# Sparse-attention softmax in a hybrid decoder trunk: scaling the attention outputs in place of the probabilities

## The chip, the core and the metric

The kernel runs on one NeuronCore of a Trainium2 chip. Five engines work side by side: TensorE (PE in the profile; its weight loads have a row of their own, PEld), VectorE (DVE), ScalarE (ACT), GpSimd (POOL) and SyncE (SP), which issues most DMA transfers. The metric is the device time of one execution in microseconds (us). The kernel before has a median of 1512.5 us in 3 runs (1512.34 to 1512.63).

## What is computed

Two decoder layers over 512 tokens of width 1024. A layer has one input projection, three head groups side by side (RWKV-7 recurrence, causal pooling, sparse attention), one output projection, a gated ConvFFN and a gated per-layer embedding. The change concerns the attention group, 8 query heads on 2 key/value heads of width 64. With 512 tokens the selected branch takes in every causal block and the window branch every causal key, so both are plain causal softmax attention with their own keys and values:

```
ps = softmax(where(ok_s, q . k_sel, -1e30));  o_sel = ps @ v_sel
pw = softmax(where(ok_w, q . k_win, -1e30));  o_win = pw @ v_win
pc = softmax(where(ok_c, q . k_cmp, -1e30)) * any(ok_c);  o_cmp = pc @ v_cmp
o  = sigmoid(g0) * o_cmp + sigmoid(g1) * o_sel + sigmoid(g2) * o_win
```

Per query and head, a causal branch thus needs its exponentials, their sum, and one factor: gate over sum.

## The kernel before, in words

Activations lie feature-major (features on partitions, the 512 tokens along the row). Large projections are made of three products of rounded halves per 128 weights, 128x512 each (lines 159 to 161).

The attention stage of a layer works on 8 units of work, one for each block `c` of 128 queries and each half `jp` of the heads. A unit has four heads: `j2` (2) times key/value head `g` (2). The stage is three pieces of code:

- `scores(c, j, pbs)`: for each `g` and branch `ty` (selected, window), two products and a causal mask go into a PSUM tile `sc` (lines 760 to 762 for c < 2, 770 to 772 for c of 2 and 3; two buffers), VectorE takes the row maximum `smax` (764, 773), and ScalarE writes the exponentials into `pb` and their row sums into `ssum` (776). Then `fac` = gate / sum (781, 782), and line 787 multiplies each `pb` by its factor, one number for each query, which here is the partition: three of four products on VectorE, one on GpSimd.
- `values(c, jp, pbs)`: TensorE transposes each 128x128 piece of the probabilities (860, PSUM tile `ptp`, two buffers of the tag `mm`), ScalarE copies four of them out as `zt` (862), and `weigh` multiplies by the values (868) into PSUM tile `o`, of which there is one. Both branches and the compressed branch (873, from `ptb`, whose probabilities carry their factor already) add up in the same 256 columns. ScalarE then writes `yh` from it (885) and VectorE the rounding rest `yl` (886).
- `pair` runs `scores` for the two heads j of a unit; the loop over `work` hands out the scores of unit i+1 while `values` of unit i is emitted.

The RWKV recurrence (lines 499 to 569) and the pooling run in the same stretch on the same engines, and the output projection `wo` follows, which reads `yh` and `yl` of all groups. What order each engine's queue has in the end is set at build time by a scheduler with its own clock; tiles come from pools with a fixed number of buffers, and a tile waits for a free one.

Of the kernel before, what the change touches and what calls it, by code (L numbers as in the profile page):

```python
# [15 lines left out]
P = 128  # L16
# [14 lines left out]
# parameter columns  # L31
PG_MIX, PG_FFN, PG_PLE, PMU, PW0, PA0, PKK, PKA, PRK, PGNG, PGNB, PSC, PC0, PC1, PC2, PCB, NPAR = (
    0, 8, 16, 24, 32, 34, 36, 38, 40, 42, 44, 46, 48, 92, 136, 180, 224)
# constant columns
C_ID, C_XM, C_BO, C_CM, C_VM, C_SEL, C_SGN, C_INV, C_HALF, C_ONE, C_FLAG, C_PIW, C_PFX, NCST = (
    0, 128, 256, 384, 512, 640, 642, 643, 644, 660, 661, 665, 667, 699)
# masks that pass through a temporary
C_DM, C_SCAN, NMSK = 0, 128, 640

# order of the feature-major tiles of the input projection  # L40
# [3 lines left out]
def hybrid(tc, xT, pT, pos, cst, msk, par, gfin, w_in, w_tok, w_out, w_up, w_down, w_pg, w_pp,  # L44
# [5 lines left out]
    with ctx:  # L50
# [85 lines left out]
        class Pace:  # L136
            """hands out the pieces of a second stream of work while the first one is emitted"""
# [17 lines left out]
        def gemm(ps, chunks):  # L155
            """chunks: list of (whi, wlo, xhi, xlo)"""
# [7 lines left out]
        def wtile(src, ps, xs, name, lo_eng=None):  # L164
            """one 128-wide tile of outputs: K chunks of weights against the list xs of (hi, lo)"""
            gemm(ps, wchunks(src, xs, lo_eng))
# [91 lines left out]
        # ================================================================  # L258
        for l in range(L):
# [5 lines left out]
            # derived parameters  # L265
# [20 lines left out]
            def mixed(i, dst):  # L286
                """token shift of tile i into dst"""
# [15 lines left out]
            # ---- RWKV: decay, a, gate  # L303
# [35 lines left out]
            # ---- normalised keys  # L339
# [12 lines left out]
            # k * (1 + (a - 1) k_a)  # L352
# [13 lines left out]
            for hp in range(2):  # L366
# [5 lines left out]
                # 2 a kk  # L372
# [5 lines left out]
            # token shift of the values  # L378
# [8 lines left out]
            # pairwise products within a chunk  # L387
# [19 lines left out]
            # the bonus  # L407
# [4 lines left out]
            # inverse of the unit triangular matrices: substitution in 32-blocks, instance on partition,  # L412
            # even columns on the lower half of the partitions and odd ones on the upper half
# [52 lines left out]
            # token-major [B|K] scaled by the chunk's decay, and V  # L466
# [24 lines left out]
            # one chunk of the recurrence  # L491
# [112 lines left out]
            # stacks of the compressed branch's inputs: even positions on the lower half, odd ones on the upper half  # L604
# [19 lines left out]
            # token-major values and gates  # L624
# [24 lines left out]
            # compressed keys and values  # L649
# [12 lines left out]
            # key stacks for the compressed branch  # L662
# [12 lines left out]
            # values of the compressed branch on (j, g, n) rows, zero outside their group  # L675
# [20 lines left out]
            # scores of the compressed branch: (head, block) on partitions, then transposed  # L696
# [47 lines left out]
            def scores(c, j, pbs):  # L744
                w = (c + 1) * P
                smax = small([P, 2, 2], "smax", 3)
                ssum = small([P, 2, 2], "ssum", 3)
# [3 lines left out]
                for g in range(2):  # L751
# [26 lines left out]
                    if g == 0:  # L778
                        yield
                fac = small([P, 2, 2], "fac", 3)  # L780
                V.reciprocal(fac, ssum)
                V.tensor_tensor(fac, fac, GT[:, c, 8:24].rearrange("p (a h) -> p h a", h=8)[:, j * 2:j * 2 + 2, :],
                                op=ALU.mult)
                for g in range(2):
                    for ty in range(2):
                        e = G if (g, ty) == (j % 2, 1) else V
                        e.tensor_scalar(pbs[g][:, ty, 0:w], pbs[g][:, ty, 0:w], fac[:, g, ty:ty + 1], None, op0=ALU.mult)
# [380 lines left out]
```

## Time and profile before

| What | Value |
|---|---|
| Time, median of 3 runs | 1512.5 us |
| Profiled execution: span from first to last instruction | 1509.1 us |
| PE busy | 1456.7 us (97%) |
| DVE, ACT, POOL busy | 824.0, 680.7, 741.9 us |
| Attention stage of layer one / two | 184 to 299.3 / 922 to 1036.5 us |

The profile names an instruction by line, engine and tile. "Busy" of PE counts modelled ends of pipelined products, so a busy PE is not one at its full rate. A wait is put down to the instruction that released it.

### The profile page before, as it was taken

How to read it: one execution, taken by the hardware profiler on the slowest of the kernel's cores; microseconds unless marked ns; L12 is line 12 of the kernel's file. 1: busy time of each engine (PE TensorE's matmuls, PEld its weight loads, DVE VectorE, ACT ScalarE, POOL GpSimd, SP SyncE). 2: the span in 40 equal slices, each digit the busy share in tenths (PEclk: the TensorE clock that was granted, in tenths of full speed). 3: DMA queues.
4: the chain of work that ended last, by engine and by line, in shares of the span. 5: the costliest groups of instructions: out<-in, count | busy, mean ns of one | idle time of the engine just before them, and what ended most of it. 6: DMA issues, size and time to landing. Idle time of an engine off the chain costs nothing.

```text
span 1509.1 us, 21414 instructions
## 1 busy us (share of the span) xinstructions
PE 1456.7 (97%) x7762; PEld 1165.4 (77%) x7762; DVE 824.0 (55%) x1362; ACT 680.7 (45%) x1302; POOL 741.9 (49%) x621
## 2 busy tenths in 40 slices
PE   6998999999999999999999989899999999999997
PEld 4786766588888888888877877656888888888886
DVE  7769687425773155522567696862277712554234
ACT  5552365544443244443544524664354423444433
POOL 3354553274555455556613554523645554555653
PEclk9999999999999999999999999999999999999998
DMA  5233400042223322333431343001322333223332
GB/s 174 67 98 93 119 16 3 15 140 89 99 92 98 103 95 95 96 97 107 137 109 55 97 126 85 1 15 57 125 91 98 94 97 102 98 98 93 97 101 94
DMA packets 79945, 134.70 MB, mean 89 GB/s; under 512 B 11104, under 2 KB 21856, under 8 KB 79840
## 3 DMA queue, kind: packets, MB, share of 16 engines
q1 hardware_dynamic: 78688, 132.29, 28.1%
q8 instruction: 61, 1.00, 0.3%
q10 hardware_dynamic: 1152, 1.05, 0.2%
q14 instruction: 44, 0.36, 0.1%
HBM read 120.59 MB, written 4.19 MB: 83 GB/s over the span
## 4 chain that ended last, share of the span: by engine, by line
PE 85%; DVE 10%; ACT 2%; issue 1%; DMA 1%; POOL 0%; SPq 0%; DVEq 0%; ACTq 0%
PE up L161 11%; PE up L160 11%; PE up L159 11%; PE dn L160 5%; PE dn L161 5%; PE dn L159 5%; PE z L161 3%; PE z L159 3%; PE z L160 3%; PE o L868 2%; PE ptp L860 2%; PE wo L159 2%; PE wo L160 2%; PE wo L161 2%; PE pg L159 2%; PE pg L160 2%
## 5 line engine op out<-in xcount | busy, mean ns | idle before, releaser
L133 POOL TENSOR_TENSOR wlo<-raw,whi 128x512 fp32r<-128x512 f32 (+3 forms) x392 | 508.0, 1300 | 478.3 <-ACT whi L132 450.8
L132 ACT CAST whi<-raw 128x512 fp32r<-128x512 f32 (+3 forms) x440 | 261.1, 596 | 437.0 <-PE up L160 111.4
L159 PE MATMUL up<-xhl,whi 128*128 128x512 f32 x704 | 274.1, 389 | 0.0
L161 PE MATMUL up<-xhl,wlo 128*128 128x512 f32 x704 | 273.7, 389 | 0.0
L160 PE MATMUL up<-xhl,whi 128*128 128x512 f32 x704 | 273.6, 389 | 0.0
L159 PEld LDWEIGHTS up<-xhl,whi 128*128 128x128 f32 x704 | 132.2, 188 | 27.4
L160 PEld LDWEIGHTS up<-xhl,whi 128*128 128x128 f32 x704 | 132.2, 188 | 27.4
L161 PEld LDWEIGHTS up<-xhl,wlo 128*128 128x128 f32 x704 | 132.2, 188 | 27.2
L159 PE MATMUL dn<-ghl,whi 128*128 128x512 f32 x352 | 136.9, 389 | 0.0
L160 PE MATMUL dn<-ghl,whi 128*128 128x512 f32 x352 | 136.9, 389 | 0.0
L161 PE MATMUL dn<-ghl,wlo 128*128 128x512 f32 x352 | 136.3, 389 | 0.0
L159 PE MATMUL z<-xhl,whi 128*128 128x512 f32 x288 | 118.1, 411 | 6.4 <-ACT whi L132 5.7
L160 PE MATMUL z<-xhl,whi 128*128 128x512 f32 x288 | 117.9, 410 | 5.6 <-DVE xhl L192 5.6
L931 DVE SCALAR_TENSOR_TENSOR cv<-cv,par 128x511 f32<-128x511 f32 x88 | 78.1, 888 | 82.0 <-ACT cv L930 82.0
L161 PE MATMUL z<-xhl,wlo 128*128 128x512 f32 x288 | 117.7, 409 | 4.9 <-DVE wlo L133 4.7
L946 DVE TENSOR_TENSOR x<-x,dn 128x512 f32<-128x512 f32 x32 | 22.0, 688 | 166.7 <-PE dn L161 166.7
L933 DVE SCALAR_TENSOR_TENSOR cv<-cv,par 128x510 f32<-128x510 f32 x88 | 100.4, 1142 | 2.9
L929 DVE TENSOR_TENSOR cv<-up,rb 128x512 f32<-128x512 f32 x88 | 60.0, 683 | 73.8 <-PE up L161 59.6
L776 ACT ACTIVATE pb<-sc,smax 128x128 f32<-128x128 f32 (+3 forms) x128 | 66.9, 531 | 41.9 <-DVE smax L764 20.3
L930 ACT ACTIVATE cv<-cv,par 128x512 f32<-128x512 f32 x88 | 71.6, 815 | 31.0 <-DVE cv L929 31.0
L159 PEld LDWEIGHTS dn<-ghl,whi 128*128 128x128 f32 x352 | 66.1, 188 | 13.8
L160 PEld LDWEIGHTS dn<-ghl,whi 128*128 128x128 f32 x352 | 66.1, 188 | 13.7
(302 smaller groups left out, 2634.4 us busy)
## 6 DMA issues: line engine op xcount, KB each, us to landing
raw<-in_w_up_dram SPq DMA_DIRECT2D x176, 256.0 KB, 2.6
raw<-in_w_in_dram SPq DMA_DIRECT2D x72, 256.0 KB, 2.8
raw<-in_w_down_dram SPq DMA_DIRECT2D x64, 256.0 KB, 2.6
raw<-in_w_out_dram SPq DMA_DIRECT2D x32, 256.0 KB, 2.7
raw<-in_w_pg_dram SPq DMA_DIRECT2D x32, 256.0 KB, 2.6
raw<-in_w_down_dram SPq DMA_DIRECT2D x32, 192.0 KB, 2.3
x<-in_xT_dram SPq DMA_DIRECT2D x16, 256.0 KB, 3.6
qs<-hl SPq DMA_DIRECT2D x32, 128.0 KB, 2.3
```

The costliest lines, as they stand in the source:

```text
L132: S.copy(hi[:, :ncol], raw[:, :ncol])
L133: (lo_eng or G).tensor_tensor(lo[:, :ncol], raw[:, :ncol], hi[:, :ncol].bitcast(F32), op=ALU.subtract)
L159: TE.matmul(ps, wh, xh, start=i == 0, stop=False)
L160: TE.matmul(ps, wh, xl, start=False, stop=False)
L161: TE.matmul(ps, wl, xh, start=False, stop=i == n - 1)
L776: S.activation(pb[:, ty, 0:w], srcs[ty], AF.Exp, bias=smax[:, g, ty:ty + 1], accum_out=ssum[:, g, ty:ty + 1])
L860: TE.transpose(ps[:, (g * 2 + j2) * P:(g * 2 + j2 + 1) * P], pbs[j2][g][:, ty, kb * P:(kb + 1) * P], ident)
L868: TE.matmul(op_[g * 64:g * 64 + 64, 0:256], VT[:, kb, ty * 128 + g * 64:ty * 128 + g * 64 + 64], pts[ty][:, g, :], start=False, stop=kb == ...
L929: V.tensor_tensor(u_, ps, rb, op=ALU.mult)
L930: S.activation(c_, u_, AF.Identity, scale=pc(PC2 + n), bias=pc(PCB + n))
L931: V.scalar_tensor_tensor(c_[:, 1:T], u_[:, 0:T - 1], pc(PC1 + n), c_[:, 1:T], op0=ALU.mult, op1=ALU.add)
L933: V.scalar_tensor_tensor(c_[:, 2:T], u_[:, 0:T - 2], pc(PC0 + n), c_[:, 2:T], op0=ALU.mult, op1=ALU.add)
```

## The change

The probabilities keep their raw exponentials: line 787 goes. One `ssum` and one `fac` tile serve the four heads of a unit. TensorE multiplies each column of `fac`, repeated 64 times as weights, by the identity, which spreads the factors along a row for all 64 partitions of a head (PSUM tile `fb` in the tag `sc` of the scores); ScalarE copies `fb` to SBUF. In `values` the two branches go to separate halves of `o`; VectorE multiplies `o` by `fb`, adds the halves and adds the compressed branch. That branch has its own products now, `oc`, for two query blocks at once, ahead of the units (PSUM tag `o`, copied by ScalarE). `ptb` moves from pool tag `x` to `p`, and `oc` takes its place. Comments go too, which shifts line numbers.

```diff
-            def scores(c, j, pbs):
+            def scores(c, j, pbs, ssum):
...
-                    if g == 0:
-                        yield
-                fac = small([P, 2, 2], "fac", 3)
-                V.reciprocal(fac, ssum)
-                V.tensor_tensor(fac, fac, GT[:, c, 8:24].rearrange("p (a h) -> p h a", h=8)[:, j * 2:j * 2 + 2, :],
-                                op=ALU.mult)
-                for g in range(2):
-                    for ty in range(2):
-                        e = G if (g, ty) == (j % 2, 1) else V
-                        e.tensor_scalar(pbs[g][:, ty, 0:w], pbs[g][:, ty, 0:w], fac[:, g, ty:ty + 1], None, op0=ALU.mult)
-                yield
+                    yield
 
             def pair(c, jp, pbs):
+                ssum = small([P, 4, 2], "ssum", 3)
                 for j2 in range(2):
                     pbs.append([])
-                    yield from scores(c, jp * 2 + j2, pbs[j2])
+                    yield from scores(c, jp * 2 + j2, pbs[j2], ssum[:, j2 * 2:j2 * 2 + 2, :])
+                fac = small([P, 4, 2], "fac", 3)
+                V.reciprocal(fac, ssum)
+                V.tensor_tensor(fac, fac, GT[:, c, 8:24].rearrange("p (a h) -> p h a", h=8)[:, jp * 4:jp * 4 + 4, :],
+                                op=ALU.mult)
+
+                fp = psum("fb", "sc")
+                for ty in range(2):
+                    for j2 in range(2):
+                        for g in range(2):
+                            TE.matmul(fp[g * 64:g * 64 + 64, (ty * 2 + j2) * P:(ty * 2 + j2 + 1) * P],
+                                      fac[:, j2 * 2 + g, ty:ty + 1].to_broadcast([P, 64]), ident, start=True, stop=True)
+                fb = unit([P, 2, 256], "fb", tag="p")
+                S.copy(fb.rearrange("p a q -> p (a q)"), fp)
+                pbs.append(fb)
...
-                ptb = unit([P, 2, 2, 2, P], "ptb", tag="x")
+                ptb = unit([P, 2, 2, 2, P], "ptb", tag="p")
...
+                oc = unit([P, 2, 2, 256], "oc", tag="x")
+                for jp in range(2):
+                    ps = psum("oc", "o")
+                    for g in range(2):
+                        TE.matmul(ps[g * 64:g * 64 + 64, :], VC[:, g * 64:g * 64 + 64], ptb[:, jp].rearrange("p c j q -> p (c j q)"),
+                                  start=True, stop=True)
+                    S.copy(oc[:, jp].rearrange("p c q -> p (c q)"), ps)
+                OC.append(oc)
...
-                            TE.matmul(op_[g * 64:g * 64 + 64, 0:256],
+                            TE.matmul(op_[g * 64:g * 64 + 64, ty * 256:(ty + 1) * 256],
...
-                for g in range(2):
-                    TE.matmul(op_[g * 64:g * 64 + 64, 0:256], VC[:, g * 64:g * 64 + 64],
-                              PTB[c // 2][:, c % 2, jp].rearrange("p j q -> p (j q)"), start=True, stop=False)
...
-                ov = op_[:, 0:256].rearrange("p (j q) -> p j q", q=P)
+                ob = small([P, 2, 256], "nacc", 1)
+                V.tensor_tensor(ob.rearrange("p a q -> p (a q)"), op_, pbs[2].rearrange("p a q -> p (a q)"), op=ALU.mult)
+                V.tensor_tensor(ob[:, 0, :], ob[:, 0, :], ob[:, 1, :], op=ALU.add)
+                V.tensor_tensor(ob[:, 0, :], ob[:, 0, :], OC[c // 2][:, jp, c % 2, :], op=ALU.add)
+                ov = ob[:, 0, :].rearrange("p (j q) -> p j q", q=P)
```

Where the queues move, place one: TensorE at the end of the first unit's scores in layer one. `tpc` are the transposes of the compressed probabilities, `yt` and `g` belong to the recurrence. Before:

```order
L760 MATMUL sc_1942<-ku_1713,qs_1412 128x256 [waits DVE_49,Activation_49]
L761 MATMUL sc_1942<-ku_1714,qs_1412 128x256
L762 MATMUL sc_1942<-cstr 128x256
L811 MATMUL tpc_2095<-cst,pcs_1682 128x128 [waits DVE_49,Activation_49]
L811 MATMUL tpc_2095<-cst,pcs_1682 128x128 x3
```

After:

```order
L759 MATMUL sc_1934<-ku_1713,qs_1412 128x256 [waits DVE_49,Activation_49]
L760 MATMUL sc_1934<-ku_1714,qs_1412 128x256
L761 MATMUL sc_1934<-cstr 128x256
L793 MATMUL fb_1950<-cst,fac_1947 64x128 [waits DVE_49,Activation_49]
L793 MATMUL fb_1950<-cst,fac_1947 64x128 x7
L815 MATMUL tpc_2094<-cst,pcs_1682 128x128 [waits Activation_49]
L815 MATMUL tpc_2094<-cst,pcs_1682 128x128 x3
```

The eight products of `fb` now stand between the last scores and `tpc`, and they wait for VectorE's `fac`.

Place two: TensorE at the end of the stage, where the last unit's values meet the output projection `wo`, whose first product with that unit's `yh` (line 159) is the last row. Before:

```order
L161 MATMUL wo_3014<-yh_689,wlo_3018 128x512
L868 MATMUL o_2888<-zt_2948,vt_921 64x256 [waits Activation_49]
L868 MATMUL o_2888<-zt_2948,vt_921 64x256
L159 MATMUL wo_2970<-yh_690,whi_2973 128x512 [waits Activation_49]
L159 MATMUL wo_3014<-yh_690,whi_3017 128x512
```

After:

```order
L161 MATMUL wo_3040<-yh_689,wlo_3044 128x512
L879 MATMUL o_2912<-zt_2970,vt_921 64x256 [waits Activation_49]
L879 MATMUL o_2912<-zt_2970,vt_921 64x256
L159 MATMUL wo_2996<-yh_690,whi_2999 128x512 [waits Activation_49]
L159 MATMUL wo_3040<-yh_690,whi_3043 128x512
```

Nothing has moved in between `o` and `wo` on TensorE. VectorE's queue for the same two last units, after:

```order
L893 TENSOR_TENSOR nacc_2892<-nacc_2892 128x256 [waits DVE_49]
L786 TENSOR_TENSOR fac_2898<-fac_2898,gt_922 128x8 [waits DVE_49]
L894 TENSOR_TENSOR nacc_2892<-nacc_2892,oc_2119 128x256 [waits DVE_49]
L898 TENSOR_TENSOR yl_693<-nacc_2892,yh_689 128x2x128 [waits Activation_49]
L892 TENSOR_TENSOR nacc_2985<-o_2912,fb_2910 128x512 [waits DVE_49,PE_49,Activation_49]
L893 TENSOR_TENSOR nacc_2985<-nacc_2985 128x256 [waits DVE_49]
L894 TENSOR_TENSOR nacc_2985<-nacc_2985,oc_2119 128x256 [waits DVE_49]
L898 TENSOR_TENSOR yl_694<-nacc_2985,yh_690 128x2x128 [waits Activation_49]
```

Three dependent instructions (892 to 894) now stand between `o` and `yl`; before, `yl_694<-o_2888,yh_690` stood alone.

## Rows read from the trace of the kernel before

**Rows 1.** Stage halves by window: start:end, length, busy PE, PEld, DVE, ACT, POOL, clock, DMA
```profile
184.00:245.00 61.00, 54.63 (x438) 39.02 (x438) 51.18 (x140) 37.87 (x124) 31.64 (x41) 0.97 0.10 29
245.00:299.30 54.30, 51.32 (x349) 31.51 (x345) 27.88 (x66) 31.24 (x75) 11.39 (x8) 1.00 0.04 11
922.00:984.00 62.00, 55.92 (x474) 39.59 (x473) 53.89 (x147) 38.52 (x125) 30.98 (x43) 1.00 0.05 15
984.00:1036.50 52.50, 50.30 (x344) 30.78 (x340) 26.52 (x62) 31.24 (x74) 10.83 (x8) 1.00 0.04 11
```
**Rows 2.** Waits from 184 to 299.3 us: total us, times, longest
```profile
PEld sc L770 <- ACT pb L776: 3.7, 6, 1.4
...
PEld ptp L860 <- DVE pb L787: 1.7, 5, 0.4
...
PEld ptp L860 <- POOL pb L787: 0.7, 2, 0.4
```
**Rows 3.** The same from 922 to 1036.5 us
```profile
PEld sc L770 <- ACT pb L776: 4.8, 9, 1.2
...
PEld ptp L860 <- DVE pb L787: 1.7, 4, 0.7
...
PEld ptp L860 <- POOL pb L787: 0.4, 1, 0.4
```
**Rows 4.** Groups of the span: out<-in xcount | busy us, mean ns | idle before, releaser
```profile
L873 PE MATMUL o<-ptb,VC 128*64 128x256 f32 x64 | 10.4, 400 | 1.9 <-DVE fac L782 0.7 <-DVE yl L886 0.6 <-ACT ptb L815 0.4
L787 DVE TENSOR_SCALAR pb<-pb,fac 128x128 f32<-128x128 f32 (+3 forms) x96 | 46.2, 533 | 0.7 <-DVE fac L782 0.2
L862 ACT COPY zt<-ptp 128x512 f32<-128x512 f32 x80 | 45.7, 587 | 36.6 <-PE o L868 20.4 <-PE ptp L860 16.2
L787 POOL TENSOR_SCALAR pb<-pb,fac 128x128 f32<-128x128 f32 (+3 forms) x32 | 40.1, 1253 | 66.5 <-DVE fac L782 48.5 <-ACT zt L862 12.4 <-DVE sb L529 4.0
L946 DVE TENSOR_TENSOR x<-x,dn 128x512 f32<-128x512 f32 x32 | 22.0, 688 | 166.7 <-PE dn L161 166.7
L782 DVE TENSOR_TENSOR fac<-fac,gt 128x4 f32<-128x4 f32 x32 | 6.4, 199 | 0.7
L781 DVE RECIPROCAL fac<-ssum 128x4 f32<-128x4 f32 x32 | 5.5, 172 | 6.0 <-ACT pb L776 5.6
```
**Rows 5.** TensorE in order of time: start, us, form, count
```profile
248.85 0.60 PE L536 MATMUL y<-sb,ar 128*64 128x128 f32 x4
...
289.01 0.71 PE L860 MATMUL ptp<-cst,pb 128*128 128x128 f32 x5
289.65 0.65 PE L868 MATMUL o<-zt,vt 128*64 128x256 f32 x4
290.24 0.66 PE L860 MATMUL ptp<-cst,pb 128*128 128x128 f32 x4
...
295.50 1.08 PE L868 MATMUL o<-zt,vt 128*64 128x256 f32 x8
```
**Rows 6.** All engines at the end of the first unit's scores
```profile
190.38 1.75 PE L811 MATMUL tpc<-cst,pcs 128*128 128x128 f32 x7 [1.54 <-ACT pb L776]
...
190.81 0.21 ACT L776 ACTIVATION_READ_ACCUMULATOR pb<-sc,smax 128x1 f32 x1
...
190.85 0.18 DVE L782 TENSOR_TENSOR fac<-fac,gt 128x4 f32<-128x4 f32 x1
```
**Rows 7.** A window just there, columns as in rows 1
```profile
190.00:200.00 10.00, 9.62 (x84) 7.81 (x84) 6.63 (x23) 7.19 (x24) 4.06 (x6) 0.83 0.09 29
```
**Rows 8.** All engines at the end of layer one's stage
```profile
298.11 0.65 PE L868 MATMUL o<-zt,vt 128*64 128x256 f32 x4
298.81 0.37 ACT L885 CAST yh<-o 128x256 fp32r<-128x256 f32 x1 [1.97 <-PE o L868]
...
299.24 0.73 PE L159 MATMUL wo<-yh,whi 128*128 128x512 f32 x2 [0.47 <-ACT yh L885]
```
**Rows 9.** VectorE: two dependent products of 128x256, one after the other
```profile
217.16 0.41 DVE L566 TENSOR_TENSOR ysq<-ysq,bo 128x256 f32<-128x256 f32 x1
217.60 0.42 DVE L567 TENSOR_TENSOR ysq<-ysq,gg 128x256 f32<-128x256 f32 x1
```

More of the change, by code (lines that the diff above doesn't have):

```diff
@@ L742, in hybrid @@
                     nc.sync.dma_start(KU[g][1][b, ty, :].bitcast(F32), hl[a, 0, :].bitcast(F32))
-            def scores(c, j, pbs):
+            def scores(c, j, pbs, ssum):
                 w = (c + 1) * P
                 smax = small([P, 2, 2], "smax", 3)
-                ssum = small([P, 2, 2], "ssum", 3)
                 ps = None
@@ L802, in hybrid @@
             pace.tick(1000.0)
-            PTB = []
+            OC = []
             for cp2 in range(2):
                 pcs, ei = PCS[cp2]
-                ptb = unit([P, 2, 2, 2, P], "ptb", tag="x")
+                ptb = unit([P, 2, 2, 2, P], "ptb", tag="p")
                 after(G.memset(ptb, 0.0), ei)
@@ L814, in hybrid @@
                     a = slice(j2 * 64, j2 * 64 + 64)
-                    S.copy(ptb[a, :, :, j2, :].rearrange("p c h q -> p (c h) q"),
-                           tps[a, :].rearrange("p (x q) -> p x q", q=P))
-                PTB.append(ptb)
+                    S.copy(ptb[a, :, :, j2, :].rearrange("p h c q -> p c h q"),
+                           tps[a, :].rearrange("p (c h q) -> p c h q", c=2, q=P))
+                oc = unit([P, 2, 2, 256], "oc", tag="x")
[6 more added lines that the diff above has]
+                OC.append(oc)
             def pooling(i):
@@ L867, in weigh @@
                         for g in range(2):
-                            TE.matmul(op_[g * 64:g * 64 + 64, 0:256],
+                            TE.matmul(op_[g * 64:g * 64 + 64, ty * 256:(ty + 1) * 256],
                                       VT[:, kb, ty * 128 + g * 64:ty * 128 + g * 64 + 64],
-                                      pts[ty][:, g, :], start=False, stop=kb == c and ty == 1)
-                for g in range(2):
-                    TE.matmul(op_[g * 64:g * 64 + 64, 0:256], VC[:, g * 64:g * 64 + 64],
-                              PTB[c // 2][:, c % 2, jp].rearrange("p j q -> p (j q)"), start=True, stop=False)
+                                      pts[ty][:, g, :], start=kb == 0 and ty == 0, stop=kb == c and ty == 1)
                 last_ = None
```

## The prediction, made before the run

> **What bounds the kernel now.** I read the page first: TensorE is busy 97% of the span. The question is therefore how much the change adds to TensorE, and how much room TensorE has in the one stage that is touched. So I cut the two attention stages into halves [rows 1]. The reader is to see two things there. TensorE is idle 61 − 54.63 = 6.4, 54.3 − 51.32 = 3.0, 62 − 55.92 = 6.1 and 52.5 − 50.30 = 2.2 us in the four halves, 17.7 us in all: no gain in these stages can be larger unless TensorE's own work shrinks. And VectorE, which the change relieves, is busy 51.18 of 61 and 53.89 of 62 us in the first halves (84% and 87%) but only about half of the second ones.
>
> Then I asked who ends TensorE's waits [rows 2, 3]. The line that the change removes, 787, ends waits of the transposes `ptp` for 1.7 + 0.7 us in layer one and 1.7 + 0.4 us in layer two: 4.5 us. The longest waits are ended by ScalarE's exponentials (3.7 and 4.8 us at line 770), where a new score tile waits for one of the two `sc` buffers. The change leaves those exponentials as they are.
>
> **What leaves VectorE and GpSimd.** Line 787 was 46.2 us of VectorE and 40.1 us of GpSimd [rows 4]. The reciprocals and `fac` products halve in number: (5.5 + 6.4)/2 = 6.0 us. In their place each of the 16 units (8 in a layer) has one 128x512 product, for which the nearest row is line 946 with 0.69 us [rows 4], and two steps of 128x256 at 0.41 to 0.42 us each [rows 9]: about 1.5 us, 24 us in all. VectorE thus loses 46.2 + 6.0 − 24 = 28 us, 14 for each layer. ScalarE gets 24 copies of 128x512 (16 `fb`, 8 `oc`) at 0.587 us, like `zt` in line 862 [rows 4]: 14 us, some 7 in a stage of 115 us in which it is busy 69 [rows 1], so I count it at nothing; where a copy delays an exponential, it costs its 0.59 us.
>
> **What TensorE gains in work: `fb`.** No row shows this operation, so I bound it by the nearest ones. A unit has 8 products, and a product of 32-bit values with 64 columns of weights runs as two passes: 16 passes of the form 128*64 by 128 columns. Line 536 has that form: four passes 0.60 us, of which about 0.27 is the run-out of the last, so (0.60 − 0.27)/3 = 0.11 us for each [rows 5]; these write into one column half, in series. Line 868, whose products alternate between the column halves as those of `fb` do, takes 0.65 us for four passes of 256 columns and 1.08 us for eight [rows 5]: 0.43 for four more, 0.11 for a pass of 256 columns, half of what one in series would take. So the halves run side by side. If `fb` does that, a unit costs 8 × 0.11 = 0.88 us and 16 units **14.1 us**; if in series, 1.76 and 28.2 us. I take the first, since line 868 is nearer in its order, and keep the second as the far end.
>
> **The compressed branch.** `oc` has the same columns as line 873 had, in half as many groups. What a group costs beyond its columns shows where transposes (128 columns of weights) and `o` (64 columns) alternate: line 868's group starts 0.64 us after the five transposes, where 5 × 0.11 = 0.55 would do, and the next transposes start 0.59 us after it, where 0.43 would do [rows 5]: 0.09 to 0.16 us for a switch. Eight groups fewer at 0.15: **−1.2 us**. The idle time before line 873 (1.9 us, [rows 4]) can go as well; it belongs to the 17.7.
>
> On this the Trainium skill has a rule that speaks against the change ("TensorEngine Tiling (Array Packing)", Tiling Modes, Key Properties): changing the tiling mode drains TensorE. The 0.15 us of the rows agrees with it in kind. By that rule every `fb` that stands between full-width scores would also pay two switches: 16 × 0.3 = 4.8 us more, and a time of 1529, an estimate from the rows; in the new order several `fb` stand beside 64-column work of the recurrence, so I leave it inside the range.
>
> **The start of the stage.** In the new order, `fb` of the first unit stands ahead of the transposes `tpc`, and it waits for the row sums of all eight score tiles, a reciprocal and the `fac` product. Before, `tpc` starts at 190.38; the last exponential's sum comes at 190.81 to 191.02 [rows 6], and 0.17 + 0.20 us [rows 4] follow, so `fb` starts near 191.5. Everything on TensorE behind it waits with it: about 1.0 us in layer one. The same place in layer two I put at 0.5, because there is less ahead of it to wait for, together **+1.5 us**. There is a danger: TensorE has already idled 1.54 us there [rows 6], and in the 10 us that follow, its granted clock is 0.83 [rows 7]; a stretch at 1.2 GHz within a mean of 0.83 of 2.4 GHz loses 1.7 us. A longer wait could lose the same once more: +1.7 at the upper end.
>
> **The end of the stage.** The last unit's values end in `o`, ScalarE writes `yh`, and the output projection waits: 0.47 us idle [rows 8]. Now three dependent VectorE steps stand in between, 0.69 + 0.41 + 0.42 us and some hundredth of start each, 1.6 us. Nothing on TensorE covers them, since `wo`'s remaining products all need this `yh`. Two layers: **+3.3 us**. The same steps in the other 14 units hold the single `o` buffer 0.7 us longer at most (the product alone reads it, then it is free, and `yh` no longer does), which I cost at nothing since transposes of the next unit cover it.
>
> **What comes back.** The lower bound is the waits on line 787 themselves, 4.5 us; the upper one is all 17.7 us. I take **−6 us**, near the lower bound: the longest waits are on exponentials and on the two `sc` buffers, and `fb` takes one more `sc` buffer per eight score tiles.
>
> **The sum.** 14.1 − 1.2 + 1.5 + 3.3 − 6 = +11.7 us. The span was 1509.1 us and the median 1512.5 us, 3.4 us outside the span that I keep: 1512.5 + 11.7 = 1524. Upper end with what was bounded: 28.2 + 1.5 + 1.7 + 3.3 − 4.5 = +30, 1542; lower end: 14.1 − 1.2 + 3.3 − 17.7 = −1.5, 1511.
>
> **The rivals.** *VectorE bounds the first halves* (the other side, faster). At 84 to 87% busy it could be that score tiles, row maxima and the recurrence all queue behind line 787, which the waits name only by whoever came last. Then 28 us less of VectorE's work empties the first halves, all 17.7 us of idle time goes, and the broken groups of transposes there (they stand in ones and twos where `pb` comes late) close up: some 3 switches for each of 8 first-half units, 24 × 0.15 = 3.6 us. With the start and `oc`'s saving: 14.1 − 1.2 + 3.3 − 17.7 − 3.6 = −5, 1507. It decides from about 13 us of recovered time on top of the 4.5 above. For it speaks VectorE's share; against it that ScalarE's exponentials end the longest waits, and that the second halves, with VectorE half idle, still show 5 us.
>
> *All idle time fills, but no more*: −1.5 to +2 us, 1511 to 1515. For it: `fb` is short and can slip into waits for exponentials. Against it: it waits itself for the last of them.
>
> *Stalls of the new order*: `fb` needs the whole unit's scores, and `o` waits longer for its product, so TensorE may come to stand before runs of score tiles with only two `sc` buffers. The waits at line 770, 1.2 to 1.4 us for the longest [rows 2, 3], are the price of one such; three or four more in each layer make +8 us, 1532.
>
> *`fb` in series*: +14 us, 1538. The Trainium skill would have it so ("TensorE: Matmul & The Clock Gate", Part 3: Packing small matmuls): a weight load overlaps products in flight only if its row groups differ, and both halves of `fb` use all 128 rows. By that rule the time is 1538; the trace disagrees as far as line 868 goes [rows 5], whose halves share all rows too and still take half the time, so it gets a small chance.
>
> *The change doesn't relieve anyone*: a scheduler could leave the idle time as it is; then −6 falls away, 1530. It belongs to the forecast's upper part.
>
> **How the numbers follow.** Forecast, 1516 to 1530: 0.50. Stalls of order, 1530 to 1536: 0.12. In series, 1536 to 1542: 0.08. All idle time fills, within 0.2% (3 us, about what can be told from no change here): 0.16. VectorE bounds, under 1509.5: 0.14. Slower by over 0.2% is then 0.70. The range of 8 in 10 reaches from 1508, inside the fast case, to 1536, where the series case begins.
>
> **What the changed profile would show.** A group of `fb` takes about 0.9 us from its first pass to the next tile's first (1.8 would mean series). VectorE is about 28 us less busy, GpSimd 40 us less. No wait of `ptp` on `pb` by VectorE or GpSimd is left. The first `wo` product with the last unit's `yh` starts some 2 us after the last `o`, not 0.5. `tpc` starts near 192.5, behind `fb`. TensorE's idle time in the halves falls from 17.7 to about 12 us and its busy time grows by some 13. I am wrong on the fast side if the first halves lose over 8 us each, and on the slow side if waits at the `sc` tiles grow beyond 10 us in a layer or the clock stays lower for long after the start.

## The result, and the profile after

The changed kernel takes 1534.6 us (median of 4 runs, 1532.5 to 1535.4) beside 1512.6 us for the kernel before: a ratio of 1.0143, with an interval of 1.0128 to 1.0158. It is 22 us slower. The forecast was 1524, the range reached to 1536; the time that came is that of a rival, the stalls of the new order (1532).

The page of the changed kernel, its first lines:

```profile
span 1532.5 us, 21696 instructions
## 1 busy us (share of the span) xinstructions
PE 1475.3 (96%) x7986; PEld 1180.3 (77%) x7986; DVE 805.5 (53%) x1282; ACT 694.5 (45%) x1326; POOL 701.3 (46%) x589
```

TensorE's share fell from 97 to 96% although it has more to do: 18.6 us more busy time in 23.4 us more span. VectorE's and GpSimd's busy time fell by 18.5 and 40.6 us. Next, windows of the two whole attention stages (from the first score product to the first `wo` product behind the last `o`; columns as in [rows 1]: start:end, length, busy PE, PEld, DVE, ACT, POOL, granted clock, DMA). The changed kernel:

```profile
185.66:316.78 131.12, 117.28 (x893) 79.19 (x892) 69.38 (x164) 76.50 (x211) 23.44 (x35) 0.95 0.06 18
938.27:1058.70 120.43, 112.69 (x911) 76.33 (x909) 71.00 (x166) 75.84 (x211) 24.18 (x36) 0.99 0.03 10
```

and the kernel before, in the same manner:

```profile
184.28:299.24 114.96, 105.61 (x782) 70.44 (x781) 79.00 (x204) 69.11 (x199) 43.03 (x49) 0.99 0.07 20
922.74:1036.50 113.76, 105.47 (x799) 69.70 (x797) 79.91 (x206) 69.76 (x199) 41.41 (x50) 1.00 0.03 11
```

The stages grew by 16.2 and 6.7 us, together 22.8 of the 23.4 us of span. In layer one TensorE is idle 13.8 us, more than before (9.4), and its granted clock is 0.95 on the mean. VectorE is 53 to 59% busy, before 69 to 70%, and yet the stage is longer.

Where the first loss arises can be read in order of time at the end of the first unit's scores (start, duration, engine, line, form, count, and in brackets the idle time before with what ended it). The changed kernel:

```profile
189.94 0.28 PE L761 MATMUL sc<-cstr 128*128 128x256 f32 x1
...
191.71 0.37 ACT L775 ACTIVATE pb<-sc,smax 128x128 f32<-128x128 f32 x1
191.96 0.21 ACT L775 ACTIVATION_READ_ACCUMULATOR pb<-sc,smax 128x1 f32 x1
...
192.20 0.20 DVE L785 RECIPROCAL fac<-ssum 128x8 f32<-128x8 f32 x1 [1.42 <-ACT pb L775]
192.44 0.17 DVE L786 TENSOR_TENSOR fac<-fac,gt 128x8 f32<-128x8 f32 x1
...
192.75 1.97 PE L793 MATMUL fb<-cst,fac 128*64 128x128 f32 x16 [2.54 <-DVE fac L786]
...
194.66 1.12 PE L815 MATMUL tpc<-cst,pcs 128*128 128x128 f32 x4
```

The last score product starts at 189.94. Behind it TensorE stands for 2.54 us until the last exponential's sum (192.17), the reciprocal and the `fac` product are done; `fb` runs, and `tpc`, which needs none of this, starts behind it at 194.66. Before it started at 190.38 [rows 6]. That `fb` takes 1.9 us to the next tile's first pass here and 1.0 elsewhere is the clock: it runs at 1.2 GHz, half of 2.4, from 192.3 to 195.7 us.

Further on the same thing returns in another dress. Score tiles of the sixth unit, TensorE alone:

```profile
259.59 0.22 PE L771 MATMUL sc<-cstr 128*128 128x128 f32 x1
260.71 0.44 PE L769 MATMUL sc<-ku,qs 128*128 128x384 f32 x1 [0.90 <-ACT pb L775]
...
262.74 0.44 PE L769 MATMUL sc<-ku,qs 128*128 128x384 f32 x1 [0.49 <-ACT pb L775]
...
264.89 0.69 PE L560 MATMUL yt<-cst,yc 128*128 128x128 f32 x2 [1.48 <-DVE yc L557]
265.51 1.97 PE L854 MATMUL pool<-pz,wpool 64*64 64x512 f32 x4
267.80 1.98 PE L793 MATMUL fb<-cst,fac 128*64 128x128 f32 x16 [0.31 <-DVE fac L786]
```

Scores follow each other with nothing between them, each waiting for one of the two `sc` buffers; TensorE idles, and then the clock falls to 1.2 GHz: `fb` takes 1.91 us to the next tile in place of 1.02. In the stages the lower of the two levels lasts 13.7 and 3.4 us, before 3.4 and 0. The stretches in the changed kernel (columns as above; the granted clock, 0.50, is the third number from the end):

```profile
192.34:195.75 3.41, 3.00 (x21) 2.69 (x22) 1.90 (x5) 0.58 (x1) 0.80 (x1) 0.50 0.29 82
243.54:246.95 3.41, 3.41 (x17) 2.46 (x18) 1.42 (x4) 1.37 (x4) 0.00 (x0) 0.50 0.03 7
264.02:270.85 6.83, 5.64 (x25) 3.02 (x25) 3.46 (x8) 2.94 (x7) 0.54 (x1) 0.50 0.03 10
991.06:994.47 3.41, 3.27 (x9) 1.40 (x9) 2.90 (x6) 1.64 (x6) 3.22 (x5) 0.50 0.00 0
```

TensorE is busy for 15.3 of these 17.1 us. At 2.4 GHz that work would take half as long, so by this estimate the clock costs 7.7 us here and, in the same manner, 1.7 us in the kernel before: 6.0 of the 22.

The end of the stage, which was priced in the prediction:

```profile
313.93 0.65 PE L879 MATMUL o<-zt,vt 128*64 128x256 f32 x4
...
314.68 0.69 DVE L892 TENSOR_TENSOR nacc<-o,fb 128x512 f32<-128x512 f32 x1 [9.97 <-PE o L879]
315.41 0.42 DVE L893 TENSOR_TENSOR nacc<-nacc 128x256 f32<-128x256 f32 x1
315.87 0.42 DVE L894 TENSOR_TENSOR nacc<-nacc,oc 128x256 f32<-128x256 f32 x1
316.32 0.41 ACT L897 CAST yh<-nacc 128x256 fp32r<-128x256 f32 x1 [3.67 <-DVE nacc L894]
...
316.78 0.73 PE L159 MATMUL wo<-yh,whi 128*128 128x512 f32 x2 [2.21 <-ACT yh L897]
```

The three new steps stand one behind the other between `o` and `yh`, and TensorE waits 2.21 us where it waited 0.47 [rows 8].

### The profile page after: what moved, and what is told of

Read it like the earlier page. It is cut to its first block, busy times and chain, and to the rows that moved or that the text cites. A ratio compares the mean times of both kernels' runs of the same rounds, so it can differ in the third digit from the quotient of the medians.

```text
span 1532.5 us, 21696 instructions
## 1 busy us (share of the span) xinstructions
PE 1475.3 (96%) x7986; PEld 1180.3 (77%) x7986; DVE 805.5 (53%) x1282; ACT 694.5 (45%) x1326; POOL 701.3 (46%) x589
## 4 chain that ended last, share of the span: by engine, by line
PE 86%; DVE 9%; ACT 2%; issue 1%; POOL 1%; DMA 0%; SPq 0%; DVEq 0%; ACTq 0%; POOLq 0%
PE up L161 10%; PE up L160 10%; PE up L159 10%; PE dn L161 5%; PE dn L159 5%; PE dn L160 5%; PE o L879 3%; PE ptp L871 3%; PE z L161 2%; PE z L159 2%; PE z L160 2%; PE wo L159 2%; PE wo L160 2%; PE wo L161 2%; PE pg L159 2%; PE pg L160 2%
## 5 line engine op out<-in xcount | busy, mean ns | idle before, releaser
L132 ACT CAST whi<-raw 128x512 fp32r<-128x512 f32 (+3 forms) x440 | 261.2, 596 | 438.6 <-PE up L160 114.7
L161 PE MATMUL z<-xhl,wlo 128*128 128x512 f32 x288 | 117.5, 408 | 4.6 <-DVE wlo L133 4.3
L160 PE MATMUL z<-xhl,whi 128*128 128x512 f32 x288 | 117.5, 409 | 4.4 <-DVE xhl L192 4.3
L775 ACT ACTIVATE pb<-sc,smax 128x128 f32<-128x128 f32 (+3 forms) x128 | 66.8, 527 | 47.4 <-DVE smax L772 24.6
L160 PEld LDWEIGHTS dn<-ghl,whi 128*128 128x128 f32 x352 | 66.1, 188 | 13.7
L161 PEld LDWEIGHTS dn<-ghl,wlo 128*128 128x128 f32 x352 | 66.1, 188 | 13.7
```

Of the source, the lines that this page charges most:

```text
L132: S.copy(hi[:, :ncol], raw[:, :ncol])
L160: TE.matmul(ps, wh, xl, start=False, stop=False)
L161: TE.matmul(ps, wl, xh, start=False, stop=i == n - 1)
L775: S.activation(pb[:, ty, 0:w], srcs[ty], AF.Exp, bias=smax[:, g, ty:ty + 1], accum_out=ssum[:, g, ty:ty + 1])
```

## The experiments

One measure I counted from the trace: how long TensorE's scores pause between two units, that is from the start of the last score product of a unit to the start of the first one of the next, seven times in each layer. A pause is not idle time: TensorE does other work in it, `fb` too. "Stages" are the two lengths as above. All from one profiled execution each; the medians are of the timed runs.

| Kernel | Median, us | Stage of layer one, two | Pauses, layer one, two |
|---|---|---|---|
| before | 1512.6 | 115.0, 113.7 | 17.8, 10.3 |
| after | 1534.6 | 131.1, 120.4 | 42.6, 31.7 |
| e1 before without the scaling | 1499.4 | 107.6, 107.9 | 16.6, 12.7 |
| e2 after without `fb` | 1502.4 | 108.8, 110.6 | 17.4, 13.2 |
| e3 after, `fb` by transposes | 1534.8 | 130.9, 121.8 | 42.0, 38.4 |
| e4 after, other buffers | 1549.2 | 130.4, 134.0 | 35.0, 37.7 |
| e5 after, late pooling product | 1553.3 | 131.7, 131.6 | 44.8, 44.5 |
| e6 e5 and transposes | 1542.1 | 128.7, 125.4 | 38.1, 37.9 |
| e7 e6 and last unit scaled | 1546.7 | 132.7, 127.4 | 39.3, 38.0 |
| e8 before, late pooling product | 1512.1 | 116.1, 112.9 | 18.5, 12.7 |
| e9 after, `fb` of a constant | 1525.6 | 117.5, 119.1 | 28.5, 29.4 |
| e10 after, `fb` made late | 1511.0 | 113.8, 114.7 | 26.0, 22.8 |
| e11 e10 and transposes | 1511.5 | 114.8, 113.4 | 25.5, 24.6 |
| e12 e10 and last unit scaled | 1511.7 | 114.0, 113.1 | 26.3, 26.0 |

The pauses tell three kinds of kernel apart: without `fb` (28 to 31 us in the two layers), with `fb` late (49 to 52) and with `fb` at the place that the change gave it (58 to 89). They do not give the time: `before` and e10 take the same with 28.1 and 48.8 us of pauses, and e4 is 14.6 us slower than the changed kernel with pauses as long.

**What the relief is worth (e1).** Line 787 is left out of the kernel before:

```diff
-                for g in range(2):
-                    for ty in range(2):
-                        e = G if (g, ty) == (j % 2, 1) else V
-                        e.tensor_scalar(pbs[g][:, ty, 0:w], pbs[g][:, ty, 0:w], fac[:, g, ty:ty + 1], None, op0=ALU.mult)
```

> The kernel before with line 787 left out (the probabilities are not scaled, the rest stays): what the relief of VectorE and GpSimd alone is worth, with nothing put in its place. The prediction's step says 6 us come back (lower bound 4.5, upper 17.7): 1506.5 us. If VectorE bounds the first halves: 1495 to 1500. If nobody waits for the scaling: 1511 to 1513.

It took 1499.4 us (ratio 0.9913, 0.9898 to 0.9928): 12.9 us come back, twice what the prediction took, near what the rival of a VectorE-bound first half says. So the gain was there, and the change had 13 us to spend. The stages in e1, columns as above:

```profile
184.50:292.10 107.60, 103.25 (x781) 69.69 (x780) 60.66 (x155) 68.88 (x199) 21.93 (x33) 0.98 0.08 21
915.10:1023.00 107.90, 103.69 (x798) 69.84 (x796) 59.91 (x157) 68.98 (x199) 21.69 (x34) 1.00 0.03 11
```

TensorE's idle time there falls from 17.6 to 8.6 us, its busy time by 4.1.

**What `fb` costs (e2).** The products and the copy go, a constant tile takes their place:

```diff
-                fp = psum("fb", "sc")
...
-                pbs.append(fb)
+                pbs.append(COS.rearrange("p (a q) -> p a q", a=2))
```

> The changed kernel without the eight products and the copy of fb (the outputs are multiplied by a constant tile instead; fac is still computed). Theory work: a group of fb took 1.02 us in the trace, 16 of them 16.3 us, and the first one waited 2.5 us: 1514 to 1518 us. Theory order (the late pooling product and the runs of score tiles with a lower clock come from the buffers and the PSUM bank that fb takes): those go too, another 6 to 8 us, 1508 to 1511.

It took 1502.4 us (0.9932, 0.9915 to 0.9949): 32 us under the changed kernel, more than either theory allowed, and only 3.0 us over e1, which is about the two tails (2 x 1.74 = 3.5). So all of the loss hangs on `fb`; its own work (16.4 us, below) is half of it. The groups of `fb` products in the changed kernel and in e10 (below), with busy time, mean, and the idle time before them:

```profile
L793 PE MATMUL fb<-cst,fac 128*64 128x128 f32 x256 | 19.7, 296 | 5.2 <-DVE fac L786 4.1 <-ACT yh L855 0.9
L793 PEld LDWEIGHTS fb<-cst,fac 128*64 128x64 f32 x256 | 15.9, 147 | 10.0 <-ACT pb L775 7.8 <-DVE fac L786 1.1 <-issue 0.6
```

```profile
L887 PE MATMUL fb<-cst,fac 128*64 128x128 f32 x256 | 17.9, 277 | 0.0
L887 PEld LDWEIGHTS fb<-cst,fac 128*64 128x64 f32 x256 | 14.7, 136 | 2.5 <-ACT pb L775 0.8 <-issue 0.6
```

From its first pass to the next tile's first, an undisturbed group takes 1.02 us: 16.4 us in all. The weight loads of the changed kernel wait 10 us, 7.8 of them until exponentials are done; those of e10 wait 2.5. TensorE itself idles 5.2 us directly before `fb` in the changed kernel, 2.54 and 1.29 of them at the two stage starts, and not at all in e10; ten of the sixteen groups of the changed kernel start without any idle time.

**Less work for TensorE at the same place (e3).** VectorE writes each factor 64 times side by side, and four full-width transposes of one pass spread them:

```diff
-                            TE.matmul(fp[g * 64:g * 64 + 64, (ty * 2 + j2) * P:(ty * 2 + j2 + 1) * P],
-                                      fac[:, j2 * 2 + g, ty:ty + 1].to_broadcast([P, 64]), ident, start=True, stop=True)
+                for i4 in range(4):
+                    TE.transpose(fp[:, i4 * P:(i4 + 1) * P], fb[:, i4 // 2, (i4 % 2) * P:(i4 % 2 + 1) * P], ident)
```

> The changed kernel with another spread: VectorE writes gate/sum 64 times side by side (one 128x512 product in place of the 128x8 one), and TensorE makes fb by four full-width transposes of one pass each in place of eight products of two passes. Theory work: 16 x (1.02 - 0.44) = 9.3 us less, and 0.5 us more at the first unit: 1525 to 1527. If a group's price lies in the waits around it and not in its passes: 1532 to 1535.

1534.8 us, no difference to the changed kernel: what is saved in passes is waited for instead. TensorE's busy time in the stages fell by 8.5 us, its idle time rose from 21.6 to 31.3.

**Is it the SBUF buffers? (e4)** The pooling's first GpSimd step came at 230.5 us in the changed kernel, at 213.4 before, and its product holds the only `o` buffer. `fb` and `ptb` had joined the pool tag `p`, from which the pooling takes its tile, so I took both out:

```diff
-                fb = unit([P, 2, 256], "fb", tag="p")
+                fb = small([P, 2, 256], "nacc", 1)
...
-                ptb = unit([P, 2, 2, 2, P], "ptb", tag="p")
+                ptb = unit([P, 2, 2, 2, P], "ptb", tag="x")
...
-                oc = unit([P, 2, 2, 256], "oc", tag="x")
+                oc = ptb.rearrange("p a c j q -> p a c (j q)")
...
-                ob = small([P, 2, 256], "nacc", 1)
+                ob = pbs[2]
```

> The changed kernel with fb out of the pool tag p (it lies in a buffer of its own that the product then overwrites) and the compressed branch written over its own probabilities, which stay in tag x: the tag p carries what it carried before. Theory order by buffers: the pooling no longer waits, the o bank is free earlier, and the runs of score tiles with TensorE idle or at half clock in layer one go: 6 to 9 us less, 1525 to 1528. Theory work: no change, 1533 to 1536; the single buffer for fb can cost a wait of its own, up to 0.5 us for each unit, 1538.

1549.2 us (1.0242, 1.0227 to 1.0258). GpSimd's first step came 10 us earlier (220.6 us), but layer one's stage stayed at 130.4 us and its pooling product at 245.8 (before the edit 246.3), so tag `p` is not what made the product late. Layer two got worse by 13.6 us; the single buffer for `fb` may have a part in that, which this run can't tell.

**Is it the late pooling product? (e5 to e8)** The product is handed out two units later, when its data are long there:

```diff
                 if i in (2, 3):
-                    pooling(i - 2)
+                    pools.append(pooling(i - 2))
+                if i in (4, 5):
+                    pools[i - 4]()
```

> The changed kernel with the pooling in two parts: its vector work is handed out where it was, its product (the PSUM tile in the tag o, of which there is one buffer) two units later. Theory late product: in layer one the values of unit 4 waited for the o bank, which the pooling's product took at 246.3 us in place of 228.1, so the scores of two units ran with nothing between them, TensorE idle and then at half clock. With the product later that goes: layer one's stage falls from 131 us to that of layer two, 120, or lower: 1518 to 1524. Rival (fb's own place in the two sc buffers is what stops the scores, wherever the pooling is): 1531 to 1535.

> The late product together with fb by four full-width transposes. Alone the transposes changed nothing (1534.8 against 1534.6 us) though they are 9 us less work for TensorE. Theory late product: they were hidden under the stall, and with the stall gone they give their 9 us: 1509 to 1515. Rival (a chain of scores, exponentials, fac, fb, copy holds the sc buffers, and TensorE's work is not what counts): within 2 us of the late product alone.

> As the one before, and the last unit of a layer is done the old way: its probabilities are scaled on VectorE and GpSimd, no fb, and one addition of the compressed branch in place of three steps between o and wo. The tail's wait was 2.2 us against 0.47 in each layer; of 1.7 us the product and one addition go (1.1), and one group of transposes (0.4 to 0.5): 3 us less than the one before for two layers. If the tail is hidden by the load of wo's weights: no difference.

> The control: the kernel before with the pooling's product two units later, nothing else. There the product came at 228 and 241 us and the runs of score tiles were short, so theory late product expects little: 1508 to 1513. If the late product gives before as much as after, it says nothing of the change: below 1505.

e5 took 1553.3 us (1.0268, 1.0251 to 1.0285), 19 us more where 11 to 17 less were expected. The theory falls: in the trace the longest run of score products with nothing between them in layer one shrank from 18 to 10, and the stage of layer one stayed as long. What e5 shows is in its windows:

```profile
184.90:316.60 131.70, 117.85 (x893) 78.95 (x892) 68.90 (x163) 76.80 (x211) 23.47 (x35) 0.96 0.06 18
945.90:1077.50 131.60, 118.11 (x893) 79.37 (x892) 68.90 (x163) 76.76 (x211) 23.47 (x35) 0.96 0.06 17
```

Both layers now have the same length to 0.1 us and the same pauses (44.8 and 44.5): TensorE's order is now the same in both layers, product for product, and layer two, which in the changed kernel had been luckier, is as long as layer one. That is 11.8 of the 19 us; most of the rest, 6.2, arose ahead of layer two's stage (587.0 in place of 580.8 us from the start of layer one's last `wo` product to the first score). The control e8 (1512.1 us, 0.9998) shows that the late product does nothing where there is no `fb`. The late pooling product was thus a companion of the long pauses, not their cause. e6 came to 1542.1 us and e7 to 1546.7; the transposes gave 11 us here and nothing in e3, and the last unit's old way lost 4.6 where 3 were to be won. None of the three shortens the pauses, and none comes near 1512.

**Is it the wait, or the place? (e9 to e11)** The pauses point to `fb`'s place: at the end of a unit's scores, in TensorE's queue between two units, in a buffer of the scores. e9 leaves it there and takes away what it waits for:

```diff
-                                      fac[:, j2 * 2 + g, ty:ty + 1].to_broadcast([P, 64]), ident, start=True, stop=True)
+                                      C[:, C_HALF:C_HALF + 1].to_broadcast([P, 64]), ident, start=True, stop=True)
```

> The changed kernel with a constant column in place of fac as the weights of fb: the same eight products, PSUM tile, copy and buffer at the same place in the program, but nothing to wait for (the outputs are not scaled by the gates). Without fb it was 1502.4 us; its own work is 16 x 1.02 = 16.4 us. Theory wait (the other 15.7 us come from fb waiting for the last exponentials of its unit, with the score tiles of the next unit behind it): 1517 to 1521. Rival buffers (they come from the score buffer and the SBUF buffer that fb occupies): 1530 to 1535.

1525.6 us (1.0094, 1.0078 to 1.0111), 9 us less: between the two theories. The trace tells why. At the first unit `fb` still stands, now for the score buffer that the exponentials must set free:

```profile
190.53 0.28 PE L761 MATMUL sc<-cstr 128*128 128x256 f32 x1
192.45 1.40 PE L793 MATMUL fb<-cst 128*64 128x128 f32 x16 [1.64 <-ACT pb L775]
193.78 1.11 PE L815 MATMUL tpc<-cst,pcs 128*128 128x128 f32 x4
```

The stages alone, and TensorE's products of `fb` with the idle time before them:

```profile
186.20:303.70 117.50, 110.89 (x893) 76.13 (x892) 67.64 (x163) 75.65 (x211) 23.77 (x35) 0.99 0.07 20
930.20:1049.30 119.10, 111.11 (x893) 74.65 (x892) 69.25 (x163) 75.91 (x211) 24.05 (x35) 1.00 0.07 19
```

```profile
L793 PE MATMUL fb<-cst 128*64 128x128 f32 x256 | 17.8, 281 | 4.1 <-ACT pb L775 3.9
```

The stages fell by 14.9 us (251.5 to 236.6), 6.9 of idle time and 8.0 of busy time; the lower clock lasts only 3.4 us now. TensorE still idles 4.1 us before `fb`, now for score buffers. 5 us were lost ahead of layer two's stage, where the work stood in another order (585.8 in place of 580.8 us, measured as for e5).

e10 keeps everything about `fb` (products, score buffer, copy, tag `p`) and moves it into the values of its own unit, behind the last transposes:

```diff
             def pair(c, jp, pbs):
...
-                fp = psum("fb", "sc")
...
-                pbs.append(fb)
+                pbs.append(fac)
...
             def values(c, jp, pbs):
...
+                fac = pbs[2]
+                fp = psum("fb", "sc")
...
+                fb = unit([P, 2, 256], "fb", tag="p")
+                S.copy(fb.rearrange("p a q -> p (a q)"), fp)
                 weigh(c, last_)
```

> The changed kernel with fb made in the values of its own unit, behind the last transposes, in place of at the end of the unit's scores; the products, the PSUM tag sc, the copy and the tag p stay. By then fac is long there. Theory wait: 1502.4 + 16.4 = 1519, 1517 to 1522, and the first transposes of a stage (tpc) start again where they did before. Rival buffers: 1530 to 1535, since fb still takes a score buffer and a buffer of tag p once in each unit.

> As the one before, with fb by four full-width transposes of a 128x512 factor tile. In the place at the end of the scores this changed nothing (1534.8). Theory wait: the saved work now counts, 16 x (1.02 - 0.44) = 9.3 us less than the one before, 1508 to 1513. Rival buffers: no difference to the one before.

e10 took 1511.0 us (0.9998, 0.9988 to 1.0007): 23.5 us less than the changed kernel by `fb`'s new place, and level with the kernel before. That is under both theories (1517 and 1530 at least): the place costs more than theory wait had it, and `fb`'s own work less. Its stages:

```profile
185.76:299.50 113.74, 107.59 (x893) 74.72 (x892) 69.77 (x163) 75.80 (x211) 24.58 (x35) 1.00 0.07 20
920.60:1035.30 114.70, 109.73 (x910) 75.66 (x908) 69.15 (x166) 75.73 (x211) 23.93 (x36) 1.00 0.03 9
```

The counts of TensorE's instructions are those of the changed kernel, 893 in layer one; the stage is 17 us shorter, and the clock is full all through. By the two traces the stages lose 10.4 us of idle time (21.6 to 11.2) and 12.7 us of busy time, of which the clock can account for the 7.7 above; the other 5 us of busy time I can't assign.

Where in the stage the time goes is seen at the first score product of the fifth unit, in layer one of the kernel before, of the changed kernel and of e10:

```profile
217.88 0.44 PE L770 MATMUL sc<-ku,qs 128*128 128x384 f32 x1
```

```profile
234.29 0.44 PE L769 MATMUL sc<-ku,qs 128*128 128x384 f32 x1
```

```profile
225.76 0.42 PE L769 MATMUL sc<-ku,qs 128*128 128x384 f32 x1
```

From the stage's first score that is 33.6, 48.6 and 40.0 us, in layer two 32.1, 44.7 and 37.3. From there to the stage's end it is 81.4, 82.5 and 73.8 us, in layer two 81.7, 75.7 and 77.4. Against the kernel before, the changed kernel is late by 15.0 and 12.6 us when the fifth unit begins and loses next to nothing, or wins some back, behind it; against e10 layer one loses as much again behind it (8.6 and 8.7 us), layer two does not.

 At the end of the first unit's scores, where `fb` stood, there is now work that waits for little:

```profile
190.05 0.28 PE L761 MATMUL sc<-cstr 128*128 128x256 f32 x1
190.17 0.38 PE L863 MATMUL ptp<-cst,pb 128*128 128x128 f32 x2
191.42 0.33 PE L863 MATMUL ptp<-cst,pb 128*128 128x128 f32 x1 [0.87 <-ACT pb L775]
191.77 0.66 PE L807 MATMUL tpc<-cst,pcs 128*128 128x128 f32 x4
```

e11 (1511.5 us, 1.0000, 0.9987 to 1.0014) was expected 9 us under e10 and is level with it; cheaper spreading is worth nothing here either. TensorE's busy time in the stages is 6.4 us less and its idle time 17.3 us against 11.2: the passes saved turn into waiting.

**Under both kernels? (e12)** With `fb` late, the last unit of each layer is done the old way: scaled probabilities, no `fb`, one addition before `yh`.

```diff
+                    if (c, jp) == work[-1]:
...
+                                e.tensor_scalar(pbs[j2][g][:, ty, :], pbs[j2][g][:, ty, :], fac[:, g, ty:ty + 1], None,
+                                                op0=ALU.mult)
```

> The kernel with fb behind the last transposes (1511.0 us), and the last unit of each layer done the old way: probabilities scaled on VectorE and GpSimd, both branches in the same half of o, no fb, and one addition of the compressed branch before yh. Expected from the traces so far: the wait before the first wo that needs this yh falls from 2.15 to 0.96 us and one group of fb (1.0 us) goes, in two layers 4.4 us: 1506 to 1508, under both kernels. If the scaling of the last unit's eight probability tiles makes its transposes wait (in the combination with the late product something near wo waited 1.9 us): 1510 to 1513.

1511.7 us (0.9999, 0.9990 to 1.0008): no gain that can be told. The tail did fall to 0.96 us, but the last unit's transposes now wait for the scaling, and the stages give 1.4 us of the 4.4 that were expected. Layer two's stage began 4.2 us later after layer one's last `wo` product than in e10 (584.5 against 580.3 us), in a stretch where nothing was edited:

```profile
283.71 1.19 PE L875 MATMUL ptp<-cst,pb 128*128 128x128 f32 x4 [0.37 <-DVE pb L792]
...
297.28 0.74 PE L159 MATMUL wo<-yh,whi 128*128 128x512 f32 x2 [0.96 <-ACT yh L914]
```

I found no version that beats the kernel before.

## Why the prediction was right in direction and short in size

The experiments give a sum of measured differences in place of the predicted one: relief 1512.3 → 1499.4, −12.9 (e1); the three steps at the tail and what else the new output arithmetic takes, +3.0 (e2 less e1); `fb` at a place where it need not wait, +8.6 (e10 less e2); `fb` at the place that the change gave it, +23.5 (after less e10). Together +22.2; each kernel stands in this chain once with plus and once with minus, so that the sum comes out is no test of the parts. By the ratios to the runs of the kernel before beside them the four are −13.2, +2.9, +10.0 and +21.9, so a part is known to about 1.6 us.

That the time fell into the range is in part luck. The place of `fb` was taken 22 us too low; the relief was taken 6.9 us too low and the work of `fb` 5.5 us too high, which made up for some of it. Of the prediction's own signs, TensorE's idle time in the stages was to fall from 17.7 to 12 us and rose to 21.6.

- **"What comes back", taken at −6.** Half of what came: 12.9. I took the waits that name line 787 (4.5 us, [rows 2, 3]) as the nearer bound, because the longest waits named the exponentials. But an exponential waits for its row maximum, and that stood in VectorE's queue behind line 787: the one who releases last hides the one who made it late. The traces bear this out: from the end of a tile's last score product to the start of its row maximum it is 0.55 us on the mean before and 0.15 in e1, and TensorE's idle time before score products falls from 7.0 to 3.7 us. The 84 to 87% of VectorE in [rows 1] were the better guide. The rival on VectorE went too far with 17.7 + 3.6 us; its sum also names the start, whose 1.5 us are not in it.
- **"The start of the stage", +1.5.** The mechanism was right and its price too small. `tpc` starts 9.0 us after the first score in layer one (before 6.1) and 7.0 us in layer two (before 4.8): +2.9 and +2.2; in layer one `fb` itself runs at half clock there. The real miss is that I had priced one wait at the start of each layer and nothing for what its place does afterwards: `fb` stands behind the scores of every unit, and with all of them moved away 23.5 us go. Of its direct waits TensorE shows only 5.2 us; the rest is other idle time, the clock (7.7 us by the estimate above) and some 5 us of busy time. This is the step that failed: +1.5 where 23.5 belonged.
- **The rival "stalls of the new order"**, with 12% and 1532 us, came near the sum. It named `fb`'s need of the whole unit's scores, which the runs bear out, but let the time be lost before runs of score tiles behind the late `o` buffer. TensorE's idle time directly before score products is 7.0 us in the stages of both kernels, a single wait for exponentials there is 0.9 us at most where 1.2 to 1.4 were priced, and e5 shortened these runs without any gain.
- **"`fb`", 14.1 us.** 16.4: a group takes 1.02 us, not 0.88, where it begins and ends with a switch between forms; in e10 it takes 1.02 us between transposes and 0.87 between products of `o` (236.26 to 237.14 us), so the two switches cost 0.15 us together, half of what [rows 5] would have it. The halves do run side by side; in series it would be 1.8 us and more. By the Trainium skill ("TensorE: Matmul & The Clock Gate", Part 3: Packing small matmuls) a weight load overlaps products in flight only where the row groups differ, so that the halves would run in series. The trace disagrees again, with 1.02 us for a group. That the work alone was not what counts is shown by e10, where 16.4 us of it cost 8.6 while TensorE's idle time in the stages fell from 16.0 us (e2) to 11.2, and by e3 and e11, where taking some of it off gave nothing.
- **The tail, +3.3.** Right: 2.21 − 0.47 = 1.74 us in each layer, 3.5.
- **`oc`, −1.2.** Too small to be read out of any difference here.
- **VectorE 28 us and GpSimd 40 us less busy.** GpSimd as forecast (40.6). VectorE by its groups 26: line 787's 46.2 and 4.7 of `fac` less, the three new steps 11.0 + 6.8 + 6.7 = 24.5 more. The page of the profile says 18.5, since it counts once where two instructions overlap at their ends; the durations of all VectorE instructions add up to 873.7 us before and 844.7 after, 29.0 less.

What stays open: how the 23.5 us divide. Without anything to wait for at the old place (e9), the stages give back 14.9 of the 23.0 us that the place costs them, by the wait and by the clock that stays up without it, and no run parts these two. Of the 8.1 us that are left, 4.1 are `fb`'s waits for a score buffer in e9's rows, but no run took that buffer away alone. And a part of every difference is the order that the build's scheduler happens to find: the stretch ahead of layer two's stage, which no edit meant to touch, varied from 580.3 to 587.0 us, and in the changed kernel itself the two layers, with the same code, differ by 10.7 us.

## What to carry to other kernels

A small product whose operand comes from the end of a chain (scores, exponentials, sums, reciprocal) belongs behind work that is ready, not at the spot where its operand is computed: in TensorE's queue it holds what stands behind it, and the loss can be larger than its own wait (here 5.2 us of 23.5), which here showed as more idle time elsewhere and as stretches at the lower clock. Before pricing what a moved step costs TensorE in passes, ask what stands behind it and how often; here the place was worth 23.5 us and its 16 us of work 8.6. And here a share of 85% on a helper engine was a better witness than the names in the list of waits, because these name the last in a chain.

## What the runs showed of the hardware that I had not expected

- Saving TensorE passes gave nothing at two places (e3 against after, e11 against e10: TensorE 8.5 and 6.4 us less busy in the stages, 0.3 and 0.5 us more time) and 11 us at a third (e6 against e5), some 3 of them between the stages: TensorE at 96% of the whole span was still the one who waits in these stages.
- The clock fell to 1.2 GHz not only at the stage's start. In the changed kernel it did so at 243.5, 264.0 and 991.1 us, in the middle of the stages. Ahead of the first, from 238 us on, TensorE had idled five times for 0.2 to 0.9 us, ahead of the second, from 260 us on, three times for 0.2 to 0.9 us, nearly all before score tiles; one such period stretched an `fb` group from 1.02 to 1.9 us. With `fb` late no such period is left in either stage.
